# Splitting weight blocks whole, and evicting two PSUM banks at once, in the expert stage of a decoder step

## The chip, the cores and the metric

The kernel runs on one core of a Trainium2 chip. The metric is the device time of one execution in microseconds. Five engines work side by side, each through its own queue in program order: TensorE (PE, matmuls; PEld are its weight loads), VectorE (DVE), ScalarE (ACT), GpSimd (POOL) and SyncE (SP, which here only issues DMAs). They wait for one another through semaphores.

## The reference

One inference step of one layer, for 256 prompt tokens and 8 sample tokens together (264 columns in the kernel), with model width 2048 and everything in float32:

```python
proj = x @ w_in                      # split into the inputs and gates of two branches
y_a, ... = ssd_branch(...);  y_b, new_sc = shortconv_branch(...)
mix = jax.nn.sigmoid(g_a) * (y_a @ w_branch_ssd) + jax.nn.sigmoid(g_b) * (y_b @ w_branch_sc)
x1 = layer_norm(ALPHA * x + mix @ w_out, ln1_g, ln1_b)
x2 = layer_norm(ALPHA * x1 + peer(x1, peer_wq, peer_keys1, peer_keys2, peer_u, peer_v), ln2_g, ln2_b)
y = x2 + jax.nn.sigmoid(x2 @ ple_gate_w) * (p @ ple_proj_w)
```

`peer` is the expert stage. A query `x @ w_q` is scored against two sets of 128 keys in each of 8 heads; the best 16 of the 16 x 16 pairs choose 16 of 16384 experts. The result is the sum over the chosen experts of gate times `gelu(x . u)` times `v`, where `u` and `v` are rows of two tables of 16384 x 2048.

## The kernel before

**Weights as a stream.** All weights come in blocks of 128 x 2048 float32 (1 MB), in one fixed order over the whole kernel: the projections, then 16 blocks for q, 128 blocks of the table u, 8 x 16 blocks of the table v, 2 ple blocks and 16 output blocks. SP fetches them into three buffers `w` (L146). A float32 product is made from fp32r matmuls of parts: ACT copies the upper part of a weight (`whi`, L158), and DVE subtracts it from the weight (`wlo`, L159). Both work on halves of 1024 columns. There are four half slots for `whi` and four for `wlo`, handed out and given back first in, first out (`hifree`, `lofree`); the expert stage adds a fifth (`whi4`, `wlo4`). `next_half` fetches ahead and splits every half for which a slot is free; it is called at the start of each half block.

**The early stages** use `col_block`: 264 columns, three matmuls a weight tile (L242 to L244), results in one of four PSUM banks under the tag `mm`. The 16 q blocks belong to them. Their results are emptied by a product with the norm's scale (`np`, L977 on DVE).

**The expert stage.** For 208 of the 264 token columns all 16384 experts are computed densely; for the other 56 the chosen rows are gathered (GpSimd's indirect DMAs at L1274, DVE products at L1344 and L1354). `pair_block` multiplies one weight block with a pair of operands of 208 columns each side by side (upper and lower part, 416 columns, L278 and the last at L281) and the lower part of the weight with 208 (L279). A U block (`u_evac`) has its result folded: ACT copies one half of the bank to `as` (L1388), DVE adds the other (L1389); after every second block the pair goes through Gelu and to DRAM. While the U blocks run, background work finds the experts: top-k searches on DVE (L1072 to L1077), the selection (`sel`, `slt`) and one-hot matrices multiplied on TensorE (`gps`, L1263), the gate weights, stored to DRAM by `g_d` (L1255). After U comes `to_v`: `residual` copies x1 into 16 accumulators on ACT (L1478), and `prep` builds products of gates and hidden values as operands `co`. Each of the 8 V chunks adds its 16 blocks to the accumulators on DVE (L1457 for the first chunk, L1459); the last chunk folds them (L1461) and passes each to the second norm (`n2.add`).

**The end.** `ple_half` multiplies two blocks into 16 tiles `pj` (L1536 to L1538); then the 16 output blocks follow.

**What sets the order.** The program is written in one order by hand (a manual schedule) and each engine takes its instructions in that order. Background work sits in generators; after each half block `tick` runs as many steps of them as a budget allows. `defer(n, f)` runs f after n ticks, `soon` after one or two. A deferred step and the blocks between therefore stand in a fixed order on each queue.

## Time and profile before

| | |
|---|---|
| median of 3 runs | 2587.89 us (2587.34 to 2588.53) |
| profiled execution | 2585.9 us, span 2584.1 us |
| granted TensorE clock, mean | 0.995 |
| TensorE busy | 2558.3 us, 99% |
| VectorE busy | 2041.8 us, 79% |
| ScalarE busy | 1432.3 us, 55% |
| GpSimd busy | 602.5 us, 23% |
| moved by DMA | 688.90 MB, mean 267 GB/s |

A busy time is a sum over the whole span. It hides that the stages have different loads, so the shares are to be read stage by stage: the q blocks end near 1145 us, the U blocks fill the time to about 1833, the V blocks the time to about 2463. A group row of the page names line, engine, operation and tiles, then count, busy time and mean length in ns of one, then the idle time of the engine ahead of it and what ended it.

### The profile page before, as it was taken

The numbers are of one execution on the slowest core, as the hardware profiler recorded it, in microseconds if no ns is written. First come the engines' busy times: TensorE is split into PE (matmuls) and PEld (weight loads), VectorE is DVE, ScalarE is ACT, GpSimd is POOL, SyncE is SP. The second block draws the span as 40 slices with busy tenths as digits, with TensorE's granted clock in tenths as the row PEclk, the third lists the DMA queues.
The fourth block names the chain that finished last, engine by engine and source line by source line (L and its number), as shares of the span: only waits on it lengthen the run. The fifth ranks groups of instructions, "written<-read, shape, count | busy, mean of one in ns | idle before, by whom it ended". The sixth has DMA issues, their size and how long they took to land.

```text
span 2584.1 us, 47957 instructions
## 1 busy us (share of the span) xinstructions
PE 2558.3 (99%) x19049; PEld 2537.6 (98%) x19049; DVE 2041.8 (79%) x3296; ACT 1432.3 (55%) x2206; POOL 602.5 (23%) x720
## 2 busy tenths in 40 slices
...
GB/s 226 228 292 276 251 177 175 182 180 179 181 180 180 180 180 180 177 182 211 226 246 361 362 359 358 354 356 381 377 381 382 368 379 369 373 350 353 205 189 123
DMA packets 137104, 688.90 MB, mean 267 GB/s; under 512 B 15744, under 2 KB 53168, under 8 KB 63280
## 3 DMA queue, kind: packets, MB, share of 16 engines
...
q8 instruction: 149, 2.44, 0.4%
...
## 4 chain that ended last, share of the span: by engine, by line
PE 85%; DVE 7%; issue 3%; DMA 3%; ACT 2%; ACTq 0%; POOL 0%; SPq 0%; DVEq 0%; POOLq 0%
PE mm L278 23%; PE mm L244 15%; PE mm L242 15%; PE mm L243 14%; PE mm L279 12%; DVE wlo L159 3%; PE mm L281 2%; PE gps L1263 1%; DMA w<-uT 1%; ACT whi L158 1%; DVE ug L1344 0%; ACT o L1251 0%; DVE as L1389 0%; DMA w<-vP 0%; DMA h0t<-h 0%
## 5 line engine op out<-in xcount | busy, mean ns | idle before, releaser
L159 DVE TENSOR_TENSOR wlo<-w,whi 128x1024 fp32r<-128x1024 f32 x916 | 1114.2, 1222 | 391.6 <-ACT whi L158 389.0
L158 ACT CAST whi<-w 128x1024 fp32r<-128x1024 f32 x916 | 955.8, 1049 | 736.4 <-PE mm L243 283.9
L278 PE MATMUL mm<-x,whi 128*128 128x416 f32 x1920 | 594.3, 370 | 1.4 <-ACT whi L158 1.4
L278 PE MATMUL mm<-co,whi 128*128 128x416 f32 x1920 | 586.1, 367 | 0.0
L244 PE MATMUL mm<-x,wlo 128*128 128x264 f32 x1920 | 549.0, 286 | 4.8 <-DVE wlo L159 4.8
L242 PE MATMUL mm<-x,whi 128*128 128x264 f32 x1920 | 548.1, 285 | 0.0
L243 PE MATMUL mm<-x,whi 128*128 128x264 f32 x1920 | 545.9, 284 | 0.0
L279 PE MATMUL mm<-x,wlo 128*128 128x208 f32 x2048 | 511.0, 260 | 3.9 <-DVE wlo L159 3.8
L279 PE MATMUL mm<-co,wlo 128*128 128x208 f32 x2048 | 509.4, 259 | 0.5 <-DVE wlo L159 0.4
L279 PEld LDWEIGHTS mm<-x,wlo 128*128 128x128 f32 x2048 | 391.9, 191 | 7.2 <-DVE wlo L159 6.8
L279 PEld LDWEIGHTS mm<-co,wlo 128*128 128x128 f32 x2048 | 390.3, 191 | 1.5 <-DVE wlo L159 1.1
L244 PEld LDWEIGHTS mm<-x,wlo 128*128 128x128 f32 x1920 | 362.1, 189 | 5.9 <-DVE wlo L159 5.8
L278 PEld LDWEIGHTS mm<-x,whi 128*128 128x128 f32 x1920 | 362.4, 189 | 5.0 <-ACT whi L158 1.6
L242 PEld LDWEIGHTS mm<-x,whi 128*128 128x128 f32 x1920 | 362.7, 189 | 1.4 <-issue 1.4
L278 PEld LDWEIGHTS mm<-co,whi 128*128 128x128 f32 x1920 | 360.7, 188 | 2.6
L243 PEld LDWEIGHTS mm<-x,whi 128*128 128x128 f32 x1920 | 361.8, 188 | 0.0
L1250 POOL TENSOR_SCALAR o<-iot,slot,slot 128x128 f32<-128x128 f32 x156 | 189.9, 1224 | 3.7 <-issue 2.0
L1274 POOL DMA_INDIRECT ug<-vR,sidx x56 | 98.1, 1752 | 294.9 <-DVE x1s L1354 236.8
L1274 POOL DMA_INDIRECT ug<-uR,sidx x56 | 92.9, 1658 | 269.2 <-DVE ug L1344 231.9
L1344 DVE SCALAR_TENSOR_TENSOR ug<-ug,x1s 128x2048 f32<-128x2048 f32 x56 | 128.0, 2286 | 2.7 <-DMA ug<-uR,sidx 2.7
L1354 DVE SCALAR_TENSOR_TENSOR x1s<-ug,scf,x1s 128x2048 f32<-128x2048 f32 x53 | 124.2, 2344 | 0.2 <-DMA ug<-vR,sidx 0.2
L880 POOL CAST r1h<-r1gbh 128x2 fp32r<-128x2 f32 x16 | 4.4, 278 | 476.0 <-PE mm L244 476.0
...
## 6 DMA issues: line engine op xcount, KB each, us to landing
w<-uT SPq DMA_DIRECT2D x128, 1024.0 KB, 6.4
w<-vP SPq DMA_DIRECT2D x128, 1024.0 KB, 8.4
w<-w_in SPq DMA_DIRECT2D x118, 1024.0 KB, 5.0
w<-w_bc SPq DMA_DIRECT2D x16, 1024.0 KB, 4.8
w<-w_bs SPq DMA_DIRECT2D x16, 1024.0 KB, 4.9
w<-w_o SPq DMA_DIRECT2D x16, 1024.0 KB, 4.9
w<-w_q SPq DMA_DIRECT2D x16, 1024.0 KB, 4.8
w<-w_pg SPq DMA_DIRECT2D x16, 1024.0 KB, 4.9
```

Of the source, the lines that this page charges most:

```text
L158: ac.copy(hi, w)
L159: ve.tensor_tensor(lo, w, hi.bitcast(F), OP.subtract)
L242: te.matmul(ps, wh, xh[kb], start=(first and q == 0), stop=False)
L243: te.matmul(ps, wh, xl[kb], start=False, stop=False)
L244: te.matmul(ps, wl, xh[kb], start=False, stop=(last and q == n - 1))
L278: te.matmul(ps, hi[:, ws], xp[kb], start=(kb == 0), stop=False)
L279: te.matmul(ps[:, :TD], lo[:, ws], xp[kb][:, :TD], start=False, stop=False)
L281: te.matmul(ps, hi[:, ws], xp[kb], start=False, stop=True)
L1250: (gp if q < 3 else ve).tensor_scalar(o1[:, q], iot, slot[0][:, c], slot[2][:, c], OP.is_equal, OP.mult)
L1274: gp.indirect_dma_start(out=t, out_offset=None, in_=tab, in_offset=bass.IndirectOffsetOnAxis(ap=sidx[:, c:c + 1], axis=0))
L1344: ve.scalar_tensor_tensor(t, t, 1.0, x1s, OP.mult, OP.mult, accum_out=shid[:, c:c + 1])
L1354: ve.scalar_tensor_tensor(x1s, t, scf[:, c:c + 1], x1s, OP.mult, OP.add)
```

## The change

Four things change.

1. Weight slots hold whole blocks (2048 columns). In the early stages there are two of them and their halves are still split one by one, so the operations there stay as they were. From the expert stage on there is a third whole slot, and a block is split by one copy and one subtract of 2048 columns.
2. The tag `mm` moves from one pool of the whole kernel into a pool that is closed and opened anew: `mmf` for the early stages, `mme` for U and V, `mmo` for ple and output. In `mme` a tile is two banks, `[128, 2, 512]`, and there are two such tiles. Two neighbouring blocks write the two banks, and their results are evicted together at the second: the copy and the add of U over 2 x 208 columns, the add of V over 2 x 416.
3. Accumulators become 8 pairs. The second norm is called for both blocks of a pair at the odd one; in the first pair the second call is deferred by 3 ticks.
4. `o1` and `o2` have 2 buffers instead of 3, `g_mm` is deferred by 5 ticks instead of 6, the store of the gate weights by 7 instead of 8, and the scratch of dynamic DMAs is 4096 instead of 8192.

```diff
@@ -59,6 +59,19 @@
     blk = ctx.enter_context(tc.tile_pool(name="blk", bufs=1))
     dram = ctx.enter_context(tc.tile_pool(name="dram", bufs=1, space=bass.MemoryType.DRAM))
     psum = ctx.enter_context(tc.tile_pool(name="psum", bufs=1, space=bass.MemoryType.PSUM))
+    PM = {}
+
+    def open_mm(name):
+        if PM:
+            PM["stack"].close()
+        PM["stack"] = ExitStack()
+        ctx.push(PM["stack"])
+        PM["pool"] = PM["stack"].enter_context(tc.tile_pool(name=name, bufs=1, space=bass.MemoryType.PSUM))
+
+    def mm_bank(name="mm"):
+        return PM["pool"].tile([128, 512], F, name=name, tag="mm", bufs=4)
+
+    open_mm("mmf")
     ctx.enter_context(tc.manual_schedule())
 
     NBLK = 13
@@ -132,8 +145,11 @@
     wt, his, los = {}, {}, {}
     st = {"dma": 0, "split": 0}
     NW = 3
-    hifree = [wpool.tile([128, 1024], R, name=f"whi{q}") for q in range(4)]
-    lofree = [wpool.tile([128, 1024], R, name=f"wlo{q}") for q in range(4)]
+    slots = [(wpool.tile([128, 2048], R, name=f"whi{q}"), wpool.tile([128, 2048], R, name=f"wlo{q}")) for q in range(2)]
+    ring = [0, 1]
+    held = {}
+    busy = set()
+    WH = {"at": 0, "whole": False, "most": 1}
 
     def fetch(upto_i):
         while st["dma"] < min(upto_i + 1, 2 * len(order)):
@@ -145,20 +161,35 @@
             q = i % 2
             sy.dma_start(out=w[:, q * 1024:(q + n) * 1024], in_=src[:, q * 1024:(q + n) * 1024])
             for k in range(n):
-                wt[i + k] = w[:, (q + k) * 1024:(q + k + 1) * 1024]
+                wt[i + k] = w
             st["dma"] += n
 
     def split_w():
 
-        while hifree and st["split"] < 2 * len(order):
+        while st["split"] < 2 * len(order):
             i = st["split"]
-            fetch(i)
-            w = wt.pop(i)
-            hi, lo = hifree.pop(0), lofree.pop(0)
-            ac.copy(hi, w)
-            ve.tensor_tensor(lo, w, hi.bitcast(F), OP.subtract)
-            his[i], los[i] = hi, lo
-            st["split"] += 1
+            b, h = divmod(i, 2)
+            if b not in held:
+                k = ring[WH["at"]]
+                if (k, 0) in busy or (WH["whole"] and (k, 1) in busy):
+                    return
+                held[b] = k
+                WH["at"] = (WH["at"] + 1) % len(ring)
+            k = held[b]
+            n = 2 if WH["whole"] and h == 0 else 1
+            if (k, h) in busy or i + n > WH["most"]:
+                return
+            fetch(i + n - 1)
+            w = wt[i]
+            for q in range(n):
+                wt.pop(i + q)
+                busy.add((k, h + q))
+            hi, lo = (t[:, h * 1024:(h + n) * 1024] for t in slots[k])
+            ac.copy(hi, w[:, h * 1024:(h + n) * 1024])
+            ve.tensor_tensor(lo, w[:, h * 1024:(h + n) * 1024], hi.bitcast(F), OP.subtract)
+            for q in range(n):
+                his[i + q], los[i + q] = (t[:, (h + q) * 1024:(h + q + 1) * 1024] for t in slots[k])
+            st["split"] += n
 
 
     tasks = []
@@ -251,12 +282,14 @@
         return i
 
     def done_half(i):
-        hifree.append(his.pop(i))
-        lofree.append(los.pop(i))
+        his.pop(i)
+        los.pop(i)
+        b, h = divmod(i, 2)
+        busy.remove((held[b], h))
 
     def col_block(xh, xl, evac, budget=1.3, width=T):
 
-        ps = psum.tile([128, TW], F, name="mm", tag="mm", bufs=4)[:, :width]
+        ps = mm_bank()[:, :width]
         for half in range(2):
             i = next_half()
             half_mm(ps, i, range(half * 8, half * 8 + 8), xh, xl, half == 0, half == 1)
@@ -265,9 +298,12 @@
                 evac(ps)
             tick(budget)
 
-    def pair_block(xp, evac, budget):
-
-        ps = psum.tile([128, 512], F, name="mm", tag="mm", bufs=4)[:, :2 * TD]
+    def pair_block(b, xp, evac, budget):
+
+        if b % 2 == 0:
+            PM["ps"] = PM["pool"].tile([128, 2, 512], F, name="mm", tag="mm", bufs=2)
+        both = PM["ps"]
+        ps = both[:, b % 2, :2 * TD]
         for half in range(2):
             i = next_half()
             hi, lo = his[i], los[i]
@@ -280,8 +316,8 @@
                 if kb == KB - 1:
                     te.matmul(ps, hi[:, ws], xp[kb], start=False, stop=True)
             done_half(i)
-            if half == 1:
-                evac(ps)
+            if half == 1 and b % 2:
+                evac(both[:, :, :2 * TD])
             tick(budget)
 
 
...
@@ -1243,16 +1277,16 @@
             if q0 == 0:
                 GS["t"] = oh.tile([128, 128, TB], F, name="gs", tag="gs", bufs=2)
             gs = GS["t"].rearrange("p e t -> p (e t)")[:, 0:128 * tb].rearrange("p (e t) -> p e t", t=tb)
-            o1 = oh.tile([128, 4, 128], F, name="o1", tag="o1", bufs=3)
-            o2 = oh.tile([128, 4, 128], F, name="o2", tag="o2", bufs=3)
+            o1 = oh.tile([128, 4, 128], F, name="o1", tag="o1", bufs=2)
+            o2 = oh.tile([128, 4, 128], F, name="o2", tag="o2", bufs=2)
             for q in range(4):
                 c = slice(tt + q, tt + q + 1)
                 (gp if q < 3 else ve).tensor_scalar(o1[:, q], iot, slot[0][:, c], slot[2][:, c], OP.is_equal, OP.mult)
                 ac.activation(o2[:, q], iot, AF.Abs, bias=slot[1][:, c], scale=-1.0)
             ac.activation(o2, o2, AF.Relu, bias=1.0, scale=-1.0)
-            defer(6, lambda o1=o1, o2=o2, gs=gs, q0=q0: g_mm(o1, o2, gs, q0))
+            defer(5, lambda o1=o1, o2=o2, gs=gs, q0=q0: g_mm(o1, o2, gs, q0))
             if q0 + 4 == tb:
-                defer(8, lambda gs=gs, b0=b0: ac.dma_start(out=g_d[b0] if b0 < NB else gr_d, in_=gs))
+                defer(7, lambda gs=gs, b0=b0: ac.dma_start(out=g_d[b0] if b0 < NB else gr_d, in_=gs))
             yield 0.1
             yield grid(3)
         DONE["G" + str(t0)] = True
@@ -1365,8 +1399,10 @@
     raw.close()
     ab.close()
     lp = ctx.enter_context(tc.tile_pool(name="late", bufs=1))
-    hifree.append(lp.tile([128, 1024], R, name="whi4"))
-    lofree.append(lp.tile([128, 1024], R, name="wlo4"))
+    slots.append((lp.tile([128, 2048], R, name="whi2"), lp.tile([128, 2048], R, name="wlo2")))
+    ring.insert(WH["at"], 2)
+    WH["whole"] = True
+    open_mm("mme")
     tkp_stack = ExitStack()
     ctx.push(tkp_stack)
     tp = tkp_stack.enter_context(tc.tile_pool(name="topk", bufs=1))
@@ -1378,21 +1414,17 @@
 
 
     a_d = dram.tile([NE // 4, 128, 4, TD], F, name="a_d")
-    AS = {}
-
     def u_evac(e):
         def f(ps):
-            if e % 2 == 0:
-                AS["t"] = lp.tile([128, 2, TD], F, name="as", tag="as", bufs=2)
-            t = AS["t"]
-            ac.copy(t[:, e % 2], ps[:, TD:])
-            ve.tensor_tensor(t[:, e % 2], ps[:, :TD], t[:, e % 2], OP.add)
-            if e % 2:
-                def out():
-                    ac.activation(t, t, AF.Gelu)
-                    ac.dma_start(out=a_d[e // 4, :, e % 4 - 1:e % 4 + 1], in_=t)
-
-                soon(out)
+            t = lp.tile([128, 2, TD], F, name="as", tag="as", bufs=2)
+            ac.copy(t, ps[:, :, TD:])
+            ve.tensor_tensor(t, ps[:, :, :TD], t, OP.add)
+
+            def out():
+                ac.activation(t, t, AF.Gelu)
+                ac.dma_start(out=a_d[e // 4, :, e % 4 - 1:e % 4 + 1], in_=t)
+
+            soon(out)
         return f
 
     CO, ACC = {}, {}
@@ -1452,14 +1484,18 @@
 
     def v_evac(c, db):
         def f(ps):
-            a = ACC[db]
+            a = ACC[db // 2]
             if c == 0:
                 ve.scalar_tensor_tensor(a, a, ALPHA, ps, OP.mult, OP.add)
             else:
                 ve.tensor_tensor(a, ps, a, OP.add)
             if c == ECH - 1:
-                ve.tensor_tensor(a[:, :TD], a[:, :TD], a[:, TD:], OP.add)
-                n2.add(a)
+                ve.tensor_tensor(a[:, :, :TD], a[:, :, :TD], a[:, :, TD:], OP.add)
+                n2.add(a[:, 0])
+                if db > 1:
+                    n2.add(a[:, 1])
+                else:
+                    defer(3, lambda: n2.add(a[:, 1]))
         return f
 
     def finish():
...
@@ -1524,13 +1560,13 @@
             spawn(finish())
         co = [CO.pop(16 * c + e) for e in range(16)]
         for db in range(KB):
-            pair_block(co, v_evac(c, db), 1.1)
+            pair_block(db, co, v_evac(c, db), 1.1)
 
     def ple_half(q):
         i = next_half()
         hi, lo = his[i], los[i]
         for c in range(4):
-            ps = psum.tile([128, TW], F, name="mm", tag="mm", bufs=4)[:, :T]
+            ps = mm_bank()[:, :T]
             for kb in range(2):
                 sl = slice((c * 2 + kb) * 128, (c * 2 + kb) * 128 + 128)
                 te.matmul(ps, hi[:, sl], p_h[kb], start=(kb == 0), stop=False)
@@ -1554,6 +1590,7 @@
             n2.normal(j, ve)
             yield ("w", 1)
 
+    open_mm("mmo")
     while len(p_h) < 2:
         tick(1.3)
     spawn(norm2())
@@ -1657,7 +1694,7 @@
     import concourse.bacc as _bacc
     from concourse.bass_utils import run_bass_kernel_spmd as _run
 
-    nc = _bacc.Bacc("TRN2", target_bir_lowering=False, num_devices=1, dynamic_dma_scratch_size=8192)
+    nc = _bacc.Bacc("TRN2", target_bir_lowering=False, num_devices=1, dynamic_dma_scratch_size=4096)
     ins = _inputs(**{k: np.asarray(v) for k, v in inputs.items()})
     arrays, aps = {}, {}
     for name, a in ins.items():
...
```

Line numbers move by some 30 to 40: L158 and L159 become L188 and L189, L278 and L279 become L314 and L315, L977 becomes L1011, L1388 and L1389 become L1420 and L1421, L1459 and L1461 become L1491 and L1493, L1536 becomes L1572.

The order of DVE where the q blocks end and the expert blocks begin. The last `np` in each piece empties the bank of the last q block; the five rows from MAX to MAX_INDEX are one top-k search. Before:

```order
L159 TENSOR_TENSOR wlo_94<-w,whi_90 128x1024
L159 TENSOR_TENSOR wlo_13259<-w,whi_13258 128x1024
L1072 MAX tv_12034<-sv 128x8
L1073 MAX_INDEX ti_12040<-tv_12034,sv 128x8
L1075 MATCH_REPLACE sw<-tv_12034,sv 128x128
L1076 MAX tv_12034<-sw 128x8
L1077 MAX_INDEX ti_12040<-tv_12034,sw 128x8
L159 TENSOR_TENSOR wlo_97<-w,whi_93 128x1024
L1389 TENSOR_TENSOR as<-mm,as 128x208
L977 SCALAR_TENSOR_TENSOR np<-m,sgb,mm 128x264
L978 TENSOR_TENSOR np<-np,m_12123 128x264
```

and with the change:

```order
L189 TENSOR_TENSOR wlo_96<-w,whi_95 128x1024
L189 TENSOR_TENSOR wlo_13258<-w,whi_13257 128x2048
L1106 MAX tv_12033<-sv 128x8
L1107 MAX_INDEX ti_12039<-tv_12033,sv 128x8
L1109 MATCH_REPLACE sw<-tv_12033,sv 128x128
L1110 MAX tv_12033<-sw 128x8
L1111 MAX_INDEX ti_12039<-tv_12033,sw 128x8
L1011 SCALAR_TENSOR_TENSOR np<-m,sgb,mm 128x264
L1012 TENSOR_TENSOR np<-np,m_12122 128x264
```

The `np` of the last q block stood behind a third half subtract and the add of expert block 0 (L1389); now it stands ahead of them, behind one half and one whole subtract. The first matmul of expert block 0 (L314) waits for it, where before it (L278) waited only for its `whi`.

The order of ACT at the turn from U to V. `g_d` is the store of the gate weights and `acc` the copy of the residual. Before:

```order
L1388 COPY as<-mm 128x208
L1255 DMA g_d<-gs 128x4096
L158 CAST whi_91<-w 128x1024
L158 CAST whi_90<-w 128x1024
L1388 COPY as<-mm 128x208
L1478 COPY acc<-x_12220 128x416 x2
L158 CAST whi_13258<-w 128x1024
L1392 ACTIVATE as<-as 128x416
L1393 DMA a_d<-as 128x416
L1478 COPY acc<-x_12220 128x416 x2
L158 CAST whi_93<-w 128x1024
```

and with the change:

```order
L1289 DMA g_d<-gs 128x4096
L1424 ACTIVATE as<-as 128x416
L1425 DMA a_d<-as 128x416
L188 CAST whi_93<-w 128x2048
L1420 COPY as<-mm 128x416
L1515 COPY acc<-x_12219 128x416 x2
L188 CAST whi_95<-w 128x2048
L1424 ACTIVATE as<-as 128x416
L1425 DMA a_d<-as 128x416
L1515 COPY acc<-x_12219 128x416 x2
L188 CAST whi_13257<-w 128x2048
```

Between the store and the first residual copy stood two half copies and an `as` copy; now there are a Gelu with its store, one whole copy and one `as` copy of a pair.

The order of DVE ahead of the ple blocks. The last row of L1459 or L1491 in each piece is that of the last V blocks (15 before; 14 and 15 together now); L894 and L896, L906, L928 and L930, L935 and L969 belong to the second norm. Before:

```order
L159 TENSOR_TENSOR wlo_95<-w,whi_92 128x1024
L1459 TENSOR_TENSOR acc<-mm,acc 128x416
L1461 TENSOR_TENSOR acc<-acc 128x208
L872 TENSOR_TENSOR acc<-acc,pc 128x208
L935 SCALAR_TENSOR_TENSOR r_26153<-x1sp,cpar,r_26153 128x56
L159 TENSOR_TENSOR wlo_96<-w,whi_91 128x1024
L894 SCALAR_TENSOR_TENSOR r_26205<-acc,cpar,r_26205 128x208
L896 TENSOR_TENSOR da<-da,acc 128x416
L159 TENSOR_TENSOR wlo_94<-w,whi_90 128x1024
L1459 TENSOR_TENSOR acc<-mm,acc 128x416
L1461 TENSOR_TENSOR acc<-acc 128x208
L872 TENSOR_TENSOR acc<-acc,pc 128x208
```

and with the change:

```order
L189 TENSOR_TENSOR wlo_96<-w,whi_95 128x2048
L928 SCALAR_TENSOR_TENSOR r_25357<-acc,cpar,r_25357 128x208
L930 TENSOR_TENSOR da<-da,acc 128x416
L928 SCALAR_TENSOR_TENSOR r_25359<-acc,cpar,r_25359 128x208
L930 TENSOR_TENSOR da<-da,acc 128x416
L969 SCALAR_TENSOR_TENSOR r_25357<-x1sp,cpar,r_25357 128x56
L969 SCALAR_TENSOR_TENSOR r_25359<-x1sp,cpar,r_25359 128x56
L189 TENSOR_TENSOR wlo_13258<-w,whi_13257 128x2048
L1491 TENSOR_TENSOR acc<-mm,acc 128x832
L1493 TENSOR_TENSOR acc<-acc 128x2x208
L906 TENSOR_TENSOR acc<-acc,pc 128x208 x2
```

The additions of two blocks stood one block apart, each with one half subtract behind the last norm operations; now one addition for both stands behind two whole subtracts, the second directly ahead of it. The first ple matmul (L1572) waits for that addition; before, the first (L1536) waited only for its `whi`, and the third and fourth tile for the additions.

28 lines of the change are left out of this document (13 added, 15 removed).

## The prediction

> **What bounds the kernel now.** I read the page's first lines, then busy time by stretches, then what TensorE waited for.
>
> ```profile
> PE 2558.3 (99%) x19049; PEld 2537.6 (98%) x19049; DVE 2041.8 (79%) x3296; ACT 1432.3 (55%) x2206; POOL 602.5 (23%) x720
> ...
> L278 PE MATMUL mm<-x,whi 128*128 128x416 f32 x1920 | 594.3, 370 | 1.4 <-ACT whi L158 1.4
> ...
> L279 PE MATMUL mm<-x,wlo 128*128 128x208 f32 x2048 | 511.0, 260 | 3.9 <-DVE wlo L159 3.8
> ```
>
> TensorE is busy for 99% of the span, and the change leaves every matmul in place. So it can only move the time through the few stretches in which TensorE stands still, or by making new ones. In the next view a row is a stretch (us), then its length and, engine by engine, the busy time; the number behind POOL's is the granted clock.
>
> ```profile
> 1287.30:1290.70 3.40, 3.20 (x12) 3.12 (x13) 2.52 (x5) 2.99 (x8) 2.10 (x5) 0.50 0.92 307
> 1754.93:1758.34 3.41, 3.41 (x14) 3.31 (x13) 3.22 (x3) 3.41 (x6) 1.47 (x3) 0.50 0.96 336
> 2468.31:2475.14 6.83, 5.43 (x24) 5.44 (x25) 5.76 (x10) 4.09 (x11) 1.41 (x4) 0.50 0.49 173
> 1140.00:1210.00 70.00, 70.00 (x479) 68.06 (x478) 66.83 (x223) 39.96 (x69) 2.15 (x4) 1.00 0.66 217
> 1210.00:1290.00 80.00, 76.30 (x500) 75.19 (x498) 76.82 (x188) 41.08 (x58) 1.44 (x3) 0.98 0.66 215
> ...
> 1330.00:1450.00 120.00, 118.13 (x811) 116.55 (x810) 106.52 (x159) 93.01 (x163) 67.44 (x50) 1.00 0.86 328
> ...
> 1740.00:1760.00 20.00, 17.82 (x107) 17.05 (x105) 8.26 (x9) 7.94 (x13) 6.04 (x8) 0.91 0.87 328
> 1760.00:1900.00 140.00, 139.37 (x918) 136.70 (x917) 127.10 (x127) 77.81 (x103) 39.33 (x34) 1.00 0.99 387
> 1900.00:2440.00 540.00, 540.00 (x3623) 537.47 (x3623) 495.53 (x526) 263.77 (x307) 152.39 (x157) 1.00 0.92 356
> 2440.00:2470.00 30.00, 26.12 (x175) 25.62 (x174) 29.62 (x55) 18.24 (x39) 6.89 (x19) 0.97 0.53 176
> ```
>
> In 1900-2440, where most of the V blocks run, TensorE never stops. What could be won is its idle time elsewhere, length minus busy: 3.7 us where experts are selected (1210-1290; DVE busy 96%), 1.9 in 1330-1450, 2.2 at the turn to V, 0.6 in 1760-1900, 3.9 before the ple blocks. The view of waits names them (us in total, times, longest):
>
> ```profile
> PE mm L279 <- DVE wlo L159: 4.2, 5, 1.6
> PE mm L1536 <- DVE acc L1459: 3.9, 2, 3.6
> PE slt L1201 <- DVE sel L1180: 2.6, 2, 2.1
> PE mm L278 <- ACT whi L158: 1.4, 1, 1.4
> ```
>
> Behind three of these the granted clock is 0.50. A matmul then takes about twice as long, so half of the working time in these stretches is lost: 1.6, 1.7 and 2.7 us. In all 12.3 us of idling and 6.0 us of slow clock in the stage that the change touches. Before 1144 us both programs have the same operations with the same waits.
>
> **The change part by part.**
>
> Larger operations. The nearest rows for a subtract of 2048 columns and for paired evictions:
>
> ```profile
> L159 DVE TENSOR_TENSOR wlo<-w,whi 128x1024 fp32r<-128x1024 f32 x916 | 1114.2, 1222 | 391.6 <-ACT whi L158 389.0
> ...
> L1459 DVE TENSOR_TENSOR acc<-mm,acc 128x416 f32<-128x416 f32 x112 | 65.5, 585 | 7.4 <-PE mm L281 6.5
> ...
> L1389 DVE TENSOR_TENSOR as<-mm,as 128x208 f32<-128x208 f32 x128 | 46.8, 366 | 0.9 <-ACT as L1388 0.8
> ...
> L1433 DVE TENSOR_TENSOR co<-al,co 128x832 fp32r<-128x832 f32 x32 | 32.5, 1016 | 0.5 <-ACT co L1432 0.5
> ```
>
> Two halves next to each other on DVE (start, length):
>
> ```profile
> 1146.06 2.35 DVE L159 TENSOR_TENSOR wlo<-w,whi 128x1024 fp32r<-128x1024 f32 x2
> ```
>
> From 832 to 1024 columns a subtract grows by 206 ns, 1.07 ns a column, so 2048 columns take about 1.22 + 1.10 = 2.32 us, against 2.35 for the two. That is 0.03 us per block, and 0.12 where the two stand apart and each pays its own start (2 x 1.22 - 2.32). An add of 416 instead of two of 208 costs 0.58 instead of 0.73; 832 instead of two of 416 about 1.0 instead of 1.17: 0.08 us per block. DVE thus gains 0.1 to 0.2 us in each of 256 blocks, 26 to 50 us. Hidden under a busy TensorE this is worth nothing; it counts only in the stretches above.
>
> The start of the expert stage: a new wait. TensorE's first matmul of expert block 0 begins a new PSUM pool. In the changed program it waits for the add that empties the bank of the last q block (np, line 1011, before 977), which is deferred by three ticks. Before, four banks went round across the border, and block 0 took a free one:
>
> ```profile
> 1144.81 2.00 ACT L158 CAST whi<-w 128x1024 fp32r<-128x1024 f32 x2
> 1144.89 0.46 PE L278 MATMUL mm<-x,whi 128*128 128x416 f32 x1
> ...
> 1148.33 0.28 DVE L1072 MAX8 tv<-sv 128x8 f32<-128x128 f32 x1
> ...
> 1149.70 0.29 DVE L1077 FIND_INDEX8 ti<-tv,sw 128x8 uint32<-128x128 f32 x1
> ...
> 1151.31 0.48 DVE L977 SCALAR_TENSOR_TENSOR np<-m,sgb,mm 128x264 f32<-128x264 f32 x1
> ```
>
> TensorE began at 1144.89 while that add ran at 1151.31. On DVE there now stand ahead of it, after 1146.06: one half subtract (to 1147.2), one whole one, and a top-k search. The whole one needs ScalarE's whole copy, 1144.81 + 1.0 for the half ahead of it + about 2.0 = 1147.8; it ends near 1150.1. The search took 1148.33 to 1149.99, 1.66, so it now ends at 1151.7, and the add of 0.48 at 1152.2. TensorE stands still for 1152.2 - 1144.9 = 7.3 us (6.6 if the whole copy costs DVE no wait, 7.6 if the whole operations are 0.2 dearer). Nothing covers it: no other matmul stands ahead of block 0's on the engine's queue. Once lost it isn't won back, since TensorE has no idle time in 1140-1210. The stop of 2.1 us for sel was followed by 3.41 us at half clock (1287.3), those of 1.4 and 1.6 us at the turn to V by as much (1754.9), that of 3.6 us before the ple blocks by 6.83. I take 2.5 us, with bounds 1.6 and 2.7. **Together +9.8 (8.2 to 10.3).**
>
> [...]
>
> Selection, 1210-1290 (DVE-bound). DVE is relieved by 0.1 to 0.2 in each of 16 blocks, 1.6 to 3.2 us. Against it: the first matmul of a block now needs the whole subtract, where half was enough before. Where DVE is late, the block's start waits for the second half's 1.2 us too, less the saving: about 1.05. So -0.6 to -2.2 of stall, and with it perhaps the 1.6 us of slow clock; if the later start decides, a loss of 1. **I take -1.5 (-5.3 to +1).** In 1330-1450 the same two things meet at DVE 89%: **-0.3 (-1.9 to +2).**
>
> The turn to V. ScalarE's copies of the residual wait for the store of the gate weights:
>
> ```profile
> 1736.61 0.33 ACTq L1255 DMA_DIRECT2D g_d<-gs  x1
> ...
> 1750.38 0.98 ACT L1478 COPY acc<-x 128x416 f32<-128x416 f32 x2 [8.64 <-DMA g_d<-gs]
> 1751.27 1.04 ACT L158 CAST whi<-w 128x1024 fp32r<-128x1024 f32 x1
> ...
> 1752.34 1.23 DVE L159 TENSOR_TENSOR wlo<-w,whi 128x1024 fp32r<-128x1024 f32 x1 [10.19 <-ACT whi L158]
> ```
>
> Behind it the whi copy is late, then the subtract, then TensorE. The store is deferred by 7 ticks instead of 8, so it leaves about half a block, 2.4 us, earlier; but then a whole copy and a whole subtract (2.0 + 2.3) stand between the wait and the next block, instead of 1.05 + 1.23: 2.0 later. That is -0.4, and I add a third of the 1.7 us of slow clock, which may go with a shorter stop: **-1.0** (-3.9, all gone, to +2).
>
> The end of U and the beginning of V, 1760-1900, has DMA at 99%:
>
> ```profile
> w<-vP SPq DMA_DIRECT2D x17, 1024.0 KB, 9.6
> w<-uT SPq DMA_DIRECT2D x12, 1024.0 KB, 9.3
> ```
>
> A block arrives 9.5 us after its issue, there are three buffers, and one comes free when the block's last subtract is done. Before, that was 3.3 us after arrival (two copies of 1.05, the last subtract of 1.22 behind them); whole, it is 2.0 + 2.3 = 4.3. A buffer goes round in 13.8 us against 3 x 4.8 = 14.4 for three blocks: it fits, but with 0.6 us to spare and a later first matmul. **+1.5 (0 to +6).**
>
> The ple blocks:
>
> ```profile
> 2463.00 0.37 PE L281 MATMUL mm<-co,whi 128*128 128x416 f32 x1
> ...
> 2465.80 0.28 PE L1538 MATMUL mm<-pp,wlo 128*128 128x264 f32 x1
> ...
> 2469.07 0.58 DVE L1459 TENSOR_TENSOR acc<-mm,acc 128x416 f32<-128x416 f32 x1
> ...
> 2469.71 0.59 PE L1536 MATMUL mm<-pp,whi 128*128 128x264 f32 x1 [3.63 <-DVE acc L1459]
> ```
>
> Before, several ple tiles ran (to 2465.8) before one needed the bank of the last V block. Now the first needs the paired add of blocks 14 and 15, in the order behind two whole subtracts. DVE's last add began 5.7 us behind TensorE's last V matmul (2469.1 - 2463.4). The relief of 0.2 us in the six blocks in which that lag built up makes it 4.5; with the wider add of 1.0 TensorE stands for 5.5 us, where it idled for 3.9: **+1.6 (0 to +3).**
>
> Elsewhere in V the lead stays two blocks, with TensorE at 540.00 of 540: nothing. The smaller o1/o2 pools and DMA scratch have no row on which I could hang a cost; I take 0.
>
> Sum: 9.8 - 1.5 - 0.3 - 1.0 + 1.5 + 1.6 = +10.1. The profiled run took 2585.9 us, 1.8 more than its span of 2584.1, so the changed one takes 2596.0; the median of the runs shown lies 2.0 above the profiled one, so 2598.0.
>
> **The rivals.**
>
> *DVE's relief pays the start back* (not slower). If DVE is relieved enough, the stops that it causes go: -5.3 in the selection (with its slow clock), -1.9 in 1330-1450, and -2.0 at the turn to V. The selection decides: its 3.7 us and the first half's lead of 1.05 are gone if the relief is 4.75 us over 16 blocks, 0.30 each. Sum: 9.8 - 9.2, with nothing lost elsewhere, = +0.6, so 2588.5. For it: DVE at 96% in that stretch, and 0.30 is reached if a whole subtract takes 2.2 us where two separate halves took 2.44. Against it: 1.07 ns a column, by which width saves little.
>
> *The wait at the start costs nothing.* For that the last q block's add would have to be done by 1144.9, or the new pool's first banks be free ones. The other terms then leave +0.3: 2588.2; with the first rival as well 2578.7. The recorded order, in which that add stands behind the whole subtract, speaks against it.
>
> *The starved stretch decides.* If a landing takes 10.6 us instead of 9.5, a buffer's round is 14.9 us and exceeds 14.4 by 0.5 for every three blocks; over 38 blocks that is 6.3 us instead of 1.5: 2602.8. For it: DMA at 99%. Against it: TensorE idles there for only 0.6 now, and the landing of 9.5 is already that of a crowded stretch.
>
> **How the numbers follow.** A change of under 0.2%, 5.2 us, can't be told from none: faster is below 2582.7, slower above 2593.1. Forecast 0.66, with a range of its own of 2592 to 2603, so that 0.04 of it would count as no change; relief pays back 0.18, of which 0.03 goes on to faster; no wait at the start 0.07, of which 0.03 comes with that relief and is faster; starved stretch 0.09. Slower: 0.62 + 0.09 = 0.71. Same: 0.04 + 0.15 + 0.04 = 0.23. Faster: 0.03 + 0.03 = 0.06. The range reaches from the centre of the paid-back case to a little above the starved one: 2588 to 2605, which leaves out half of the first rival, the faster cases and the worst of the starved one.
>
> **What would show it.** Right: the first L314 waits 6.6 to 7.6 us for DVE's np of line 1011, with the granted clock at 0.50 behind it; the first L1572 waits for the paired acc; TensorE's idle time in the selection is 2 to 4 us. Subtracts of 2048 columns near 2.3 us. Wrong: no wait at the first expert block; or no more idle time in the selection and at the turn to V, which would bring the time back to 2588; or waits of L314 for whi behind w transfers in 1760-1900.

## The result, and the profile after

The changed kernel took 2605.8 us (median of 4 runs, 2599.4 to 2610.1) against 2588.2 before: a ratio of 1.0066 with an interval of 1.0045 to 1.0087. A second set of six runs on another chip gave 2600.1 (2594.6 to 2608.3) against 2586.2, 1.0051 (1.0035 to 1.0068). All ten together have a median of 2601.1. The kernel is slower by 0.5 to 0.7%, and its runs scatter over 15 us where those of the kernel before scatter over some 10. The profiled execution took 2610.1, with a span of 2608.0.

The page of the changed kernel, and its view of what TensorE waited for (us in total, times, longest):

```profile
PE 2565.4 (98%) x19049; PEld 2544.0 (98%) x19049; DVE 2014.5 (77%) x2888; ACT 1390.1 (53%) x1870; POOL 703.9 (27%) x720
```

```profile
PE mm L315 <- DVE wlo L189: 11.9, 7, 3.1
PE mm L314 <- DVE np L1011: 7.0, 1, 7.0
...
PE mm L1572 <- DVE acc L1491: 4.9, 1, 4.9
PE gps L1297 <- POOL o L1284: 4.8, 6, 1.4
```

DVE and ACT are busy for 27 and 42 us less, as the wider operations were to bring. But GpSimd, whose work the change does not touch, is busy for 101 us more (703.9 after 602.5), and TensorE now waits for its one-hot matrices `o`, which it never did in the profile before. Its waits for `wlo` in the expert stage rose from 4.2 to 11.9 (8.1 in the profile of the second set).

Busy time by stretches of the changed kernel; the stretches are those of the prediction, moved along by the time lost ahead of them:

```profile
1154.00:1158.00 4.00, 3.18 (x11) 3.10 (x12) 2.67 (x12) 0.00 (x0) 0.00 (x0) 0.50 0.71 285
...
1222.00:1302.00 80.00, 77.37 (x506) 76.63 (x505) 77.11 (x171) 39.08 (x34) 1.88 (x4) 0.98 0.63 217
1341.00:1461.00 120.00, 118.80 (x815) 117.47 (x814) 107.00 (x128) 92.49 (x131) 93.22 (x54) 1.00 0.91 344
1462.00:1752.00 290.00, 286.31 (x1976) 284.46 (x1976) 213.75 (x166) 224.28 (x320) 223.00 (x132) 1.00 0.93 348
1752.00:1772.00 20.00, 18.77 (x126) 18.36 (x125) 11.43 (x7) 10.12 (x11) 8.80 (x8) 1.00 0.96 358
1772.00:1860.00 88.00, 81.88 (x522) 80.39 (x521) 70.71 (x47) 47.37 (x50) 29.75 (x22) 0.96 0.96 372
...
1912.00:2463.00 551.00, 549.32 (x3674) 546.33 (x3673) 486.00 (x355) 246.87 (x198) 169.05 (x149) 1.00 0.92 352
2463.00:2493.00 30.00, 24.93 (x162) 24.13 (x161) 29.80 (x48) 16.81 (x28) 10.89 (x26) 0.96 0.57 185
```

Length minus busy time gives what TensorE idled. The selection has less of it than before (2.6 us, was 3.7), and so has the turn to V (1.2, was 2.2, now at full clock). New are 3.7 us in the late U blocks (1462-1752, GpSimd busy 223 us) and 6.1 us in 1772-1860, with a clock of 0.96 that costs about 3 us more. In the kernel before, the late U blocks had no idle time and 175 us of GpSimd:

```profile
1450.00:1740.00 290.00, 290.00 (x2009) 288.82 (x2008) 223.51 (x250) 234.91 (x404) 174.91 (x132) 1.00 0.94 358
```

A table of where the time went, worked out from the starts of each expert block's last matmul (L281 before, L317 and its like after): us by which a block is later than in the profiled execution before. Blocks 0 to 127 are U, 128 to 255 V. "Changed, second set" is the profiled execution of the second set; the last four columns are experiments below (m_halves is the mended kernel, m_whole the same with whole subtracts).

| up to block | changed | changed, second set | side_edits | start_now | m_halves | m_whole |
|---|---|---|---|---|---|---|
| 0 | 12.1 | 11.6 | -0.5 | 2.1 | 1.8 | 2.2 |
| 16 | 12.1 | 11.7 | -0.5 | 2.2 | 1.8 | 2.2 |
| 32 | 10.8 | 10.4 | -1.7 | 4.7 | 5.7 | 5.0 |
| 104 | 14.9 | 13.5 | -0.2 | 14.6 | 1.6 | 15.1 |
| 112 | 12.0 | 10.3 | -4.5 | 10.3 | -2.7 | 10.8 |
| 128 | 20.6 | 14.4 | -4.6 | 10.8 | -1.9 | 10.1 |
| 152 | 23.1 | 13.6 | -5.6 | 10.8 | -2.6 | 9.3 |
| 255 | 23.5 | 13.9 | -5.6 | 11.1 | -2.8 | 9.6 |
| end | 23.9 | 13.8 | -7.0 | 10.6 | -6.8 | 4.8 |

In the changed kernel 2.8 us of the first row arose near 193 us, in a stage that is the same in both programs: there SyncE's loads of `h0t` waited 8.3 us for another DMA (`arow<-acs_d`) instead of 4.8. The experiment side_ple has lost 2.5 us there and side_edits nothing, though their programs are the same up to the ple blocks, so this is a difference between executions and none of the change.

### The profile page after: what moved, and what is told of

It is laid out like the page before. It is cut to its first block, busy times and chain, and to the rows that moved or that the text cites. A ratio compares the mean times of both kernels' runs of the same rounds, so it can differ in the third digit from the quotient of the medians.

```text
span 2608.0 us, 46942 instructions
## 1 busy us (share of the span) xinstructions
PE 2565.4 (98%) x19049; PEld 2544.0 (98%) x19049; DVE 2014.5 (77%) x2888; ACT 1390.1 (53%) x1870; POOL 703.9 (27%) x720
## 4 chain that ended last, share of the span: by engine, by line
PE 74%; DVE 7%; POOL 7%; issue 5%; DMA 5%; ACT 2%; ACTq 0%; SPq 0%; POOLq 0%; DVEq 0%
PE mm L314 16%; PE mm L275 15%; PE mm L273 15%; PE mm L274 15%; PE mm L315 8%; POOL o L1284 5%; DVE wlo L189 3%; DMA ug<-vR,sidx 2%; POOL ug L1308 2%; DMA w<-vP 1%; PE mm L317 1%; ACT whi L188 1%; DMA al<-a_d 1%; PE gps L1297 0%; PE yS L1349 0%
## 5 line engine op out<-in xcount | busy, mean ns | idle before, releaser
L189 DVE TENSOR_TENSOR wlo<-w,whi 128x1024 fp32r<-128x1024 f32 (+1 forms) x644 | 1079.5, 1677 | 417.1 <-ACT whi L188 411.2
L188 ACT CAST whi<-w 128x1024 fp32r<-128x1024 f32 (+1 forms) x644 | 909.2, 1412 | 726.9 <-PE mm L274 263.0
L314 PE MATMUL mm<-x,whi 128*128 128x416 f32 x1920 | 597.3, 372 | 7.0 <-DVE np L1011 7.0
L314 PE MATMUL mm<-co,whi 128*128 128x416 f32 x1920 | 587.5, 368 | 0.0
L315 PE MATMUL mm<-x,wlo 128*128 128x208 f32 x2048 | 513.2, 261 | 10.0 <-DVE wlo L189 10.0
L315 PE MATMUL mm<-co,wlo 128*128 128x208 f32 x2048 | 510.3, 259 | 1.9 <-DVE wlo L189 1.9
L315 PEld LDWEIGHTS mm<-x,wlo 128*128 128x128 f32 x2048 | 393.8, 192 | 12.2 <-DVE wlo L189 12.0
L315 PEld LDWEIGHTS mm<-co,wlo 128*128 128x128 f32 x2048 | 391.1, 191 | 3.1 <-DVE wlo L189 2.6
L314 PEld LDWEIGHTS mm<-x,whi 128*128 128x128 f32 x1920 | 364.4, 190 | 10.7 <-DVE np L1011 7.3
L314 PEld LDWEIGHTS mm<-co,whi 128*128 128x128 f32 x1920 | 361.5, 188 | 2.7
L1284 POOL TENSOR_SCALAR o<-iot,slot,slot 128x128 f32<-128x128 f32 x156 | 263.5, 1695 | 7.3 <-issue 3.4
L1308 POOL DMA_INDIRECT ug<-vR,sidx x56 | 119.8, 2139 | 259.4 <-DVE x1s L1388 227.5
L1308 POOL DMA_INDIRECT ug<-uR,sidx x56 | 100.0, 1785 | 220.4 <-DVE ug L1378 178.0
L1388 DVE SCALAR_TENSOR_TENSOR x1s<-ug,scf,x1s 128x2048 f32<-128x2048 f32 x53 | 124.4, 2348 | 14.1 <-DMA ug<-vR,sidx 14.1
```

Of the source, the lines that this page charges most:

```text
L188: ac.copy(hi, w[:, h * 1024:(h + n) * 1024])
L189: ve.tensor_tensor(lo, w[:, h * 1024:(h + n) * 1024], hi.bitcast(F), OP.subtract)
L314: te.matmul(ps, hi[:, ws], xp[kb], start=(kb == 0), stop=False)
L315: te.matmul(ps[:, :TD], lo[:, ws], xp[kb][:, :TD], start=False, stop=False)
L1284: (gp if q < 3 else ve).tensor_scalar(o1[:, q], iot, slot[0][:, c], slot[2][:, c], OP.is_equal, OP.mult)
L1308: gp.indirect_dma_start(out=t, out_offset=None, in_=tab, in_offset=bass.IndirectOffsetOnAxis(ap=sidx[:, c:c + 1], axis=0))
```

## The experiments

Each kernel was timed beside the kernel before on the same chip; the numbers are medians. Kernels of one group ran on one chip. The kernel before was 2587.4, 2587.1, 2586.2, 2587.2 and 2586.8 in the five groups.

### The wait at the start of the expert stage

The first try gave block 0 the other pair of banks (start_free):

```diff
     open_mm("mme")
+    PM["pool"].tile([128, 2, 512], F, name="mm", tag="mm", bufs=2)
```

> The changed kernel with one edit: an unused first tile in the U/V PSUM pool, so that expert block 0 writes the pool's second pair of banks and doesn't wait for the last q block's np. Theory S (the new wait at the start costs its 7.0 us and some 2 to 2.5 us of slow clock behind it, and nothing wins it back): 9 to 10 us faster than the changed kernel, no PE wait for np. Rival R (the lost time lets VectorE get ahead, so that the stops in the selection grow when the wait goes): only 3 to 6 us faster, and TensorE idles 3 us or more longer in the selection. GpSimd's one-hot operations stay near 1.7 us.

Measured: 2602.5 (2599.1 to 2605.8), and the wait for `np` still 7.0 us. The edit did not do what it was to do, so it tells nothing of S and R. It does tell that the wait isn't tied to a bank: block 0 waited for the same `np` with either pair. The first tile that is written in the newly opened pool waits for the last reader of the closed one.

The second try ends the old pool's use earlier (start_now):

```diff
-            defer(3, late)
+            if j == 15:
+                late()
+            else:
+                defer(3, late)
```

> The changed kernel with one edit: the last q block's np isn't deferred by three ticks but recorded right behind its matmuls, so that the new pool's wait for it is short. (The unused first tile did not take the wait away: any first tile of the new pool waits for everything in the old one.) Theory S: the 7.0 us wait shrinks to under 1 us and the slow clock behind it goes, 8 to 10 us faster than the changed kernel, so 2596 to 2598. Rival R (the lost time had let VectorE get ahead, and stops in the selection grow in return): 3 to 6 us faster.

Measured: 2596.0 (2592.0 to 2599.5), and a wait for `np` of 0.2 us. That is 9.8 us below the first set of the changed kernel and 5 below all ten of its runs. Its profile has block 0 10.0 us earlier (+2.1 in place of +12.1), of which 0.9 were lost ahead of the stage. S holds for the start itself, but the 2596.0 must not be read as S's whole sum come true: by block 104 the profile is level with that of the changed kernel (14.6 after 14.9). Two waits took the gain back:

```profile
PE gps L1300 <- POOL o L1287: 8.8, 8, 4.5
...
PE slt L1238 <- DVE sel L1217: 2.3, 1, 2.3
```

The wait for `sel` is absent in the changed kernel, and TensorE idles 4.1 us between blocks 16 and 32 instead of 2.6: 1.5 us of R are there. The waits for GpSimd are 8.8 us where they were 4.8, with 3.4 us of slow clock behind them. It comes out ahead only behind block 104, where the changed kernel loses more in the starved stretch.

### The side edits alone

The smaller buffers and scratch and the shorter deferrals, put into the kernel before (side_edits):

> The kernel before with the side edits alone: two buffers instead of three for o1 and o2, g_mm after 5 ticks, the store of the gate weights after 7, and the smaller scratch for dynamic DMAs. If they are harmless: within 1.5 us of the kernel before, with ScalarE's wait for that store down from 8.6 us to 5 to 7. If the scratch or the two buffers cost: 2 us or more slower, with a TensorE stop near 193 us (which the changed kernel's profile has) or gps waits for GpSimd.

Measured: 2581.6 (2577.5 to 2587.8), ratio 0.9984 (0.9975 to 0.9993). They are not harmless but a gain of 5.8 us, the larger part of it at the turn to V, where the table has -4.3 between blocks 104 and 112. ScalarE's timeline in this run (start, length, instruction, idle time before it):

```profile
1731.60 0.33 ACTq L1255 DMA_DIRECT2D g_d<-gs  x1
...
1744.23 0.98 ACT L1478 COPY acc<-x 128x416 f32<-128x416 f32 x2 [2.69 <-DMA g_d<-gs]
```

The store left 9.9 us before ScalarE began to wait for it (1741.5), where it had been 5.1 us in the profile before (1736.6 to 1741.7). The wait fell from 8.6 to 2.7 us. TensorE's wait of 1.4 us for `whi` is gone, and the mean granted clock of the run is 0.999, where it was 0.995.

### One subtract or two

The copy stays whole; the subtract becomes two of 1024 columns (lo_halves), or four of 512 (lo_quarters), or two with the second half first (lo_swapped):

```diff
-            ve.tensor_tensor(lo, w[:, h * 1024:(h + n) * 1024], hi.bitcast(F), OP.subtract)
+            for q in range(n):
+                cs = slice(q * 1024, (q + 1) * 1024)
+                ve.tensor_tensor(lo[:, cs], w[:, (h + q) * 1024:(h + q + 1) * 1024], hi[:, cs].bitcast(F), OP.subtract)
```

> The changed kernel with one edit: the copy of a block stays whole (2048 columns), but its subtract on VectorE is two operations of 1024 again. Theory L (a subtract of 2.29 us shuts GpSimd out for its whole length, so that one-hot matrices and gathers come late): the one-hot operations fall from 1.70 us back to about 1.2 us, the 4.8 us of gps waits for them go, the gathers are issued earlier and the starved stretch around the turn to V loses 6 us or more of its 10: 8 to 13 us faster than the changed kernel. Rival W (what costs is that a block's first matmul needs the whole block's copy and subtract, and that a buffer comes free later): 0 to 4 us faster only, since the buffer still waits for copy and both subtracts; the starved stretch stays. The 7.0 us wait for np stays under both.

> The changed kernel with a whole copy and the subtract in four operations of 512 columns. Theory L (GpSimd is shut out for the length of one subtract): one-hot operations at or below the 1.33 us that they took with halves, 1.1 to 1.3, gathers issued in less than 1.6 us on average, and a time within 3 us of the variant with halves (2592.9), better if the lock-out was what was left of it. If instead the sum of VectorE's work shuts GpSimd out, whatever its length: 1.33 us or more and no gain over halves, with VectorE some 20 us busier.

> As the variant with a whole copy and two half subtracts (2592.9), but the second half's subtract comes first. A block's first matmul then needs both, as with one whole subtract, while GpSimd still gets in after 1.2 us. Theory L (a long subtract shuts GpSimd out): 2590 to 2596, one-hot operations near 1.33 us, no or few gps waits for GpSimd. Rival F (what the halves won back is that a first matmul needs half a subtract only): 2601 to 2608, with TensorE's waits for wlo at 10 us or more as in the changed kernel.

And halves throughout, in copy and subtract, with all the rest of the change kept (halves_paired: `WH["whole"]` stays False, and splits run five half blocks ahead):

> The changed kernel with copies and subtracts of 1024 columns throughout, five half blocks ahead as in the kernel before; paired evictions, pools, side edits kept. Theory L and rival W both: one-hot operations at 1.2 us, the starved stretch as in the kernel before: 10 to 14 us faster than the changed kernel, that is 2592 to 2597, with the 7.0 us wait for np left over. Against lo_halves: under L the two are within 3 us of each other, under W this one is 6 us or more faster.

And the whole split without the paired evictions and the new pools, on the side edits (whole_unpaired):

> The kernel before with the side edits and with whole copies and subtracts in the expert stage (three whole slots), but single banks, single evictions, no new pools. Theory L and rival W: the whole split costs 10 to 14 us over the side edits alone (2581.6), so 2591 to 2596, with one-hot operations near 1.7 us, gps waits, and stops in the starved stretch. Rival P (the paired evictions, which free two banks at once, make those stops): 2581 to 2586.

| | median us | one-hot on GpSimd, mean us | waits for `wlo`, expert stage | gps waits for GpSimd |
|---|---|---|---|---|
| changed, six runs | 2600.1 | 1.69 | 8.1 | 4.0 |
| lo_halves | 2592.9 | 1.33 | 6.1 | none |
| halves_paired | 2593.5 | 1.40 | 3.0 | 2.0 |
| lo_quarters | 2597.4 | 1.32 | 5.8 | none |
| lo_swapped | 2598.1 | 1.36 | 9.4 | none |
| side_edits | 2581.6 | 1.33 | 2.4 | 2.3 |
| whole_unpaired | 2588.1 | 1.79 | 7.0 | 4.1 |

The medians come from three chips, lo_halves, halves_paired and side_edits from one, lo_quarters and whole_unpaired from another, the changed kernel and lo_swapped from the third. lo_halves is level with halves_paired: the whole copy on ScalarE costs nothing, the whole subtract on VectorE does, some 8 us by all ten runs of the changed kernel, and 6.5 without pairing. One part of L did not come true: the starved stretch did not go with the whole subtract. Between blocks 112 and 128 TensorE idles 4.0 us in lo_halves, where it was 6.1 and 4.5 in the two profiles of the changed kernel, and only 0.5 in halves_paired. whole_unpaired, whose 2588.1 lies between its theories, idles 4.1 us there too, so the paired evictions (P) don't make these stops either. Quarters did not shorten the one-hot operations further, against L's stronger form. They took 4.5 us more than halves, on another chip, with VectorE busy for 2067.5 us (2028.0 with halves, 2014.5 in the changed kernel). lo_swapped came out between its theories, with a gain of only 2 us on its chip, and left open whether GpSimd (L) or the later first half (F) was the cause.

The one-hot matrices moved to VectorE (onehot_dve):

```diff
-                (gp if q < 3 else ve).tensor_scalar(o1[:, q], ...)
+                ve.tensor_scalar(o1[:, q], ...)
```

> The changed kernel with the one-hot matrices o1 built on VectorE alone (117 operations of about 0.37 us move from GpSimd to it). Theory L: the 4.8 us of gps waits for GpSimd go; the gathers, still issued by GpSimd, stay late, so the stops around the turn to V stay: 2 to 7 us faster than the changed kernel. If GpSimd's lateness isn't what costs: no faster, or slower by the 43 us of added VectorE work where it is near its limit (2606 to 2612).

Measured: 2596.4 (2593.0 to 2597.1), 3.7 us below the changed kernel on its chip; the gps waits are gone. (The operations that moved are 156, not 117.) The waits bear out L's one-hot part; the time alone does not, as the changed kernel's own runs there span 2594.6 to 2608.3.

### The costs put apart on a base without the wait at the start

The mended kernel has three edits: `np` of the last q block at once, two half subtracts behind a whole copy, and ple tiles in banks of the background pool (the pool `mmo` is opened behind them). The last was first tried on the side edits (side_ple):

```diff
-            ps = psum.tile([128, TW], F, name="mm", tag="mm", bufs=4)[:, :T]
+            ps = bank("ple")[:, :T]
```

> The side edits alone (2581.6) with one more edit: the ple tiles take PSUM banks of the background pool, so none waits for the eviction of the last V blocks. The 3.9 us wait for acc goes: 3 to 6 us faster than the side edits alone, 2576 to 2579. If VectorE's lag at the end only moves (the norm waits for the same additions): 0 to 2 us.

Measured: 2579.9 (2577.6 to 2584.1), 1.7 us below the side edits, on another chip, and with ranges that overlap. The wait for `acc` is gone; in its place stands one for ScalarE's copies `pj` (3.3 us). So most of the stop only moved.

> The changed kernel with three edits: np of the last q block at once, two half subtracts behind a whole copy, ple tiles in banks of the background pool. If the three costs are separate and add up: 2592.9 less 9.8 for the start and 2 to 3 for the ple blocks, 2580 to 2582, level with the side edits alone (2581.6). If the halves' gain hung on the time lost at the start: 2584 to 2590.

Measured: 2581.1 (2576.9 to 2584.2), ratio 0.9976 (0.9968 to 0.9985). From lo_halves that is -11.8. In the profiles the two kernels are 8.7 us apart at block 0 (9.8 without what each lost ahead of the stage) and still 8.7 at block 255; the other 3 us lie behind, at the ple blocks, whose wait for `acc` was 5.8 us in lo_halves and 3.9 in the side edits. So with half subtracts the start's whole cost, 9 to 10 us, reaches the end, as S has it; with whole ones, in start_now, it did not.

On this base, on one chip, the subtract was varied alone (m_halves is the mended kernel again):

> The mended kernel with one subtract of 2048 columns again. If the whole subtract costs what it does in the changed kernel: 6 to 10 us over the mended one (2581.1), 2587 to 2591, with one-hot operations near 1.7 us, gps waits of 4 us or more, and waits for wlo of 3 to 6 us more.

> The mended kernel with its two half subtracts in swapped order, so that the first matmul needs both, while GpSimd gets in between them. Theory L alone: level with the mended kernel (within 1.5 us). Theory F alone: level with m_whole. Both: in between; from the first look (lo_swapped) 4 to 6 us over the mended kernel, with gps waits for GpSimd below 1 us and waits for wlo 3 to 6 us above the mended kernel's 3.2.

> m_whole with the one-hot matrices on VectorE alone. Theory L: gps waits go, 3 to 5 us faster than m_whole. Theory F: not faster than m_whole, or slower by VectorE's added work.

| | median us | range | ratio to the kernel before |
|---|---|---|---|
| m_halves | 2582.8 | 2578.6 to 2586.5 | 0.9982 (0.9972 to 0.9991) |
| m_swapped | 2582.8 | 2580.2 to 2586.6 | 0.9985 (0.9975 to 0.9994) |
| m_whole | 2591.3 | 2584.7 to 2594.3 | 1.0014 (1.0005 to 1.0023) |
| m_onehot | 2578.9 | 2576.0 to 2579.6 | 0.9966 (0.9954 to 0.9978) |

This settles it. m_swapped, in which a first matmul needs both halves, is level with m_halves, so F is out. The whole subtract costs 8.5 us, and all of it goes when GpSimd builds no one-hot matrices, though the subtract is whole: m_onehot is 12.4 below m_whole, where 3 to 5 were expected. That is about what m_whole loses by GpSimd, these waits and 3.4 us of slow clock:

```profile
PE gps L1300 <- POOL o L1287: 8.9, 9, 4.5
```

m_halves and m_swapped have no such wait. m_onehot has the lowest median of the study, though side_ple, the kernel before with small edits only, is 1.0 us away on another chip. m_whole shows the cause in a few rows: GpSimd, then VectorE, then TensorE, each with start and length.

```profile
1699.67 9.85 POOL L1287 TENSOR_SCALAR o<-iot,slot,slot 128x128 f32<-128x128 f32 x2
```

```profile
1699.42 2.34 DVE L1391 SCALAR_TENSOR_TENSOR x1s<-ug,scf,x1s 128x2048 f32<-128x2048 f32 x1
1701.68 2.28 DVE L189 TENSOR_TENSOR wlo<-w,whi 128x2048 fp32r<-128x2048 f32 x1
1703.88 0.39 DVE L1287 TENSOR_SCALAR o<-iot,slot,slot 128x128 f32<-128x128 f32 x1
1704.47 2.29 DVE L189 TENSOR_TENSOR wlo<-w,whi 128x2048 fp32r<-128x2048 f32 x1 [0.20 <-ACT whi L188]
1706.68 2.35 DVE L1391 SCALAR_TENSOR_TENSOR x1s<-ug,scf,x1s 128x2048 f32<-128x2048 f32 x1
```

```profile
1709.58 1.22 PE L1300 MATMUL gps<-o,o 128*128 128x128 f32 x4 [4.49 <-POOL o L1287]
```

Two one-hot operations took 9.85 us beside these four wide VectorE operations (2.28 to 2.35 us each); the next three took 2.35 together, 0.78 each. TensorE stood for 4.49 us until they were done and then took 0.59 us for a `whi` matmul that had taken 0.37, with a mean granted clock of 0.72 from 1704 to 1716; block 104 is 7.0 us further behind the kernel before than block 96.

Two last runs asked whether width and pairing bring anything. m_onehot_halves is m_onehot with two half subtracts; side_ple_onehot is side_ple with the one-hot matrices on VectorE.

> m_onehot (2578.9) with two half subtracts. If the whole subtract is harmless once GpSimd builds no one-hot matrices, and saves little: within 1.5 us of m_onehot. If its width is worth something where VectorE is near its limit: 2 us or more slower than m_onehot.

> The kernel before with the side edits, the ple tiles in background banks, and the one-hot matrices on VectorE; halves, single evictions, one pool. If width and pairing bring nothing on a busy TensorE: 2577 to 2580, within 1.5 us of m_onehot. If VectorE's relief of 0.1 to 0.2 us a block matters where it now carries the one-hot matrices as well: 2 us or more slower than m_onehot.

Measured: m_onehot_halves 2580.4 (2578.2 to 2583.9), 1.5 us above m_onehot, which on another chip can't be told from none. side_ple_onehot 2584.6 (2581.5 to 2587.4), 4.2 us above m_onehot_halves on the same chip, 5.7 above m_onehot and 4.7 above side_ple. Its TensorE waits for `wlo`:

```profile
PE mm L279 <- DVE wlo L159: 6.8, 11, 1.6
```

Eleven stops, where side_ple has 3 of 2.3 us in all. So with one-hot matrices on VectorE the relief by whole copies, wider evictions or both is worth some 4 us; with GpSimd building them it brought nothing in the time that these runs show (m_halves 2582.8, side_ple 2579.9).

## Why the prediction was right or wrong

The direction and the first cause were right, the size was not: 2598.0 with a range to 2605 was forecast, and 2605.8 measured, 2601.1 over all ten runs. The increase was forecast as 10.1 and was 17.6 in the first set, 13.9 in the second.

**The start of the expert stage: right.** Forecast were a wait of 6.6 to 7.6 us and an end of `np` near 1152.2 on the clock of the profile before. DVE and PE in the changed kernel:

```profile
1150.50 2.29 DVE L189 TENSOR_TENSOR wlo<-w,whi 128x2048 fp32r<-128x2048 f32 x1 [0.42 <-ACT whi L188]
...
1154.29 0.47 DVE L1011 SCALAR_TENSOR_TENSOR np<-m,sgb,mm 128x264 f32<-128x264 f32 x1
```

```profile
1154.82 0.71 PE L314 MATMUL mm<-x,whi 128*128 128x416 f32 x1 [7.05 <-DVE np L1011]
```

With the 2.8 us that were lost earlier taken off, `np` ends at 1152.0. Block 0 is 12.1 - 2.8 = 9.3 us late: 7.0 of waiting and 2.2 of slow clock, where 9.8 was forecast. The rival by which free banks could hide this wait had no footing: start_free took the other banks and waited as long.

**The prices: right.** By form, in the changed kernel:

```profile
L189 DVE TENSOR_TENSOR wlo<-w,whi 128x2048 fp32r<-128x2048 f32 x272 | 625.1, 2298 | 171.1 <-ACT whi L188 166.9 <-ACT sgb L1009 3.2
L188 ACT CAST whi<-w 128x2048 fp32r<-128x2048 f32 x272 | 519.6, 1911 | 372.0 <-PE mm L317 222.6 <-DMA w<-vP 94.6 <-DMA w<-uT 27.0
...
L1491 DVE TENSOR_TENSOR acc<-mm,acc 128x832 f32<-128x832 f32 x56 | 57.2, 1021 | 9.8 <-PE mm L317 9.7
...
L1421 DVE TENSOR_TENSOR as<-mm,as 128x416 f32<-128x416 f32 x64 | 37.3, 583 | 4.1 <-ACT as L1420 4.0
```

2.30 us was forecast as 2.32, 1.02 as 1.0, 0.58 as 0.58.

**The selection: right in size, the reason not shown.** Between blocks 16 and 32 the changed kernel gained 1.3 us for the forecast 1.5. Its idle time there fell from 3.7 to 2.6 us, as VectorE's relief was to bring. whole_unpaired, with wide splits and no late start, idles 2.9 us. But start_now and m_whole have all of the relief without the late start, and idle 4.1 us; side_edits has none of it and gained 1.1, by a stop with no slow clock behind it. How much was relief and how much the late start, which lets VectorE get ahead, stays open, and the match in size is partly luck. In 1330-1450 about nothing happened, as forecast, but as the sum of two things: between blocks 32 and 64 lo_halves gained 2.9 us, where the changed kernel, with its waits for GpSimd, lost 0.7.

**The turn to V: too small a gain.** The forecast let the store leave one half block, 2.4 us, earlier, and added 2.0 for the whole copy and subtract: -1.0. In the side edits alone it left 4.8 us earlier (9.9 - 5.1) and the turn gained 4.3. In the changed kernel the turn gained 2.8 (blocks 104 to 112). The 2.0 was fair; the lead was short by half. In the profile of the side edits four half copies stand between the store and the first residual copy, where there were two, so one tick less moved it by two half blocks. Why by two, the runs don't show.

**What failed: "Hidden under a busy TensorE this is worth nothing; it counts only in the stretches above."** The sum priced a wider VectorE operation by its length on VectorE alone, put its cost to others at nothing, and asked nowhere who stands still beside it. GpSimd does. The profile before already held the sign. In it, and in the changed kernel:

```profile
L1250 POOL TENSOR_SCALAR o<-iot,slot,slot 128x128 f32<-128x128 f32 x156 | 189.9, 1224 | 3.7 <-issue 2.0
```

```profile
L1284 POOL TENSOR_SCALAR o<-iot,slot,slot 128x128 f32<-128x128 f32 x156 | 263.5, 1695 | 7.3 <-issue 3.4
```

156 equal operations with a mean of 1.22 us, of which half took 0.81 or less: something stretched the others. Sorted by how long a `wlo` subtract ran beside them, those with under 0.25 us of it took 0.83 on the mean, those with about 1 us 1.63. In the changed kernel those with about 2 us took 2.67 (21 of them), and 4.41 if a product for gathered rows (`x1s` or `ug`, 2.3 to 2.5 us long) ran beside them too (19, with 4.0 us of both). That is the others' time and 0.4 to 0.7 us more. Where the one-hot operation had begun 0.05 us or more ahead of a whole subtract, with no other wide VectorE operation running, it kept its 0.79 (22 of them), and the subtract took up to 2.62 instead of 2.29. All 38 that began while a whole subtract ran took 2.03 us or more and ended at least 0.66 us behind it. So the lengths show that the one that begins second is held up; by what, they don't show. The sum missed a term of +4.0 between blocks 32 and 104 (the gps waits of 4.8); against lo_halves, which has no such wait and gained 3.0 there, it is 7.0. With the start mended the whole subtract costs 8.5 us in all (m_whole and m_halves).

**The starved stretch: the sign was right, the size and the cause were not.** Forecast were +1.5 (0 to +6), from a buffer's round of 13.8 us. The profiled execution lost 8.6 us between blocks 112 and 128 and 2.5 more up to 152, in the second profile 4.1 and -0.8. m_swapped has the same copy and frees its buffers as late, and loses 0.4 us up to block 152; m_whole, whose copy and subtract are both whole, loses nothing there (0.2 us of idle time between blocks 112 and 128). So a buffer's round alone does not make these stops, and neither does the whole subtract, as lo_halves has 4.0 us of them without it. The changed kernel's four stops between blocks 112 and 152 are all waits for `wlo`. What the changed kernel's trace shows beside them are late gathers, here the first with a whole subtract beside it and, behind it, VectorE waiting for gathered rows with the next `wlo` queued:

```profile
1810.73 2.29 DVE L189 TENSOR_TENSOR wlo<-w,whi 128x2048 fp32r<-128x2048 f32 x1 [0.20 <-ACT whi L188]
...
1817.63 2.35 DVE L1388 SCALAR_TENSOR_TENSOR x1s<-ug,scf,x1s 128x2048 f32<-128x2048 f32 x1 [3.18 <-DMA ug<-vR,sidx]
1819.90 2.28 DVE L189 TENSOR_TENSOR wlo<-w,whi 128x2048 fp32r<-128x2048 f32 x1
```

```profile
1811.13 2.74 POOL L1308 DMA_INDIRECT ug<-vR,sidx  x1 [6.39 <-DVE x1s L1388]
```

In all, `x1s` waited 14.1 us for gathers (0.2 before), 6.9 in lo_halves, 4.3 in m_whole and 0.8 in m_onehot. That these waits make the stops is what the traces suggest; it isn't shown by an experiment, and what makes the gathers late stays open, since GpSimd takes longer to issue m_onehot's gathers from table v (2.37 us on the mean, 2.14 in the changed kernel), and they cost it nothing visible. How often a late gather meets a crowded DMA may be why the changed kernel's runs scatter by 15 us; that stays open.

**The ple blocks: right**, +1.0 from block 248 to the end for +1.6 (+0.3 in the second profile), with a wait of 4.9 us where 5.5 was forecast.

Added up, in the profiled execution: 2.8 before the expert stage, 9.3 at its start, -1.3 in the selection, +4.0 of GpSimd, -2.8 at the turn, 8.6 and 2.5 in the starved stretch, and under 1 in all for the rest, 23.9. The two large misses are the 4.0 of GpSimd, which experiments show, and 9.6 of the 11.1 in the starved stretch, whose cause stays open. In the second profile they are 3.1 and 1.8.
